# Two more projections of a decoder layer join the seven-product stage of the gates, and the memory norm moves

## The chip, the cores and the metric

The kernel runs on one core of a Trainium2 chip. The metric is the device time of one launch in microseconds (us), lower is better. The engines named below: PE multiplies matrices (TensorE; its weight loads are listed as PEld), DVE works on vectors (VectorE), ACT evaluates functions and scaled copies (ScalarE), POOL is the general engine (GpSimd), SP issues most DMAs. PE writes to PSUM banks, from which ACT or DVE take the results. Each engine works through its own queue in order and waits on semaphores for the others.

## The reference, cut to what matters

One layer of a decoder on 1024 tokens of width 1024, float32. After a feed-forward half step, one input projection gives u, v (512 columns each), the latent parts of branch B, q_mem (512) and three gates (1024 each). Branch A gates u spatially with v, branch B is causal latent attention, branch C attends to 256 memory tokens with 4 heads of 128; the gated branches are projected and added, and a second feed-forward half step follows.

```
h = rmsnorm(x, mix_norm)
z = h @ w_in                     # [u | v | c_q | c_kv | k_rope | q_mem | gate_A | gate_B | gate_C]
u = gelu(z[..., u]);  v = layernorm(gelu(z[..., v]))
y_a = u * (tril(w_s) @ v + b_s)  # in chunks of 128 tokens, 8 groups of 64 columns
q   = rmsnorm(z[..., q_mem] by head, q_norm)
kv  = rmsnorm(mem, mem_norm) @ w_kv;  k = rmsnorm(kv[:512] by head, k_norm);  v = kv[512:]
y_c = softmax(q k^T * 128**-0.5) v
gates  = sigmoid(z[..., gates] + b_gate)
merged = gates_A*(y_a @ w_branch_a) + gates_B*(y_b @ w_branch_b) + gates_C*(y_c @ w_branch_c)
```

## The kernel before

**Products.** Every large product is three PE matmuls (`mm3`, L141): each operand is split into a high part (an ACT cast, L127) and a low part (a DVE subtraction, L128), and hi·hi, hi·lo and lo·hi are added in one PSUM bank. A product needs the low part too, so it waits for ACT and then DVE.

**Seven products for four.** The feed-forward layers and the gates go through class `Seven`, which makes a 2x2 block product from seven block products instead of eight, and pays with additions of blocks on DVE and POOL. In the gates' stage (`Gates`) a unit is two blocks of 128 columns over all tokens and takes 84 matmuls of 512 columns; 12 units make the 3 x 8 gate blocks. `emit` applies a sigmoid and stores each finished block, features in partitions and tokens along the row, to DRAM (`gate`).

**After the gates**, `mixer` runs latent attention's projections, then `sgu`: for each half of the tokens v (96 matmuls, `gelu_rows`), its Gelu on ACT and its LayerNorm on DVE (L625 to L631; its inverse root is a chain of small Newton steps, `rs_y`, L154 to L165); then for each half u (96 matmuls more), the spatial product with `sg_w` (24 matmuls of 256 columns), `u <- (product + b) * u` on DVE (L643) and 16 transposes with a split into `x4`. Tokens stand in partitions until those transposes.

**Memory.** `mem_kv` loads the memory into `m_x`, sums its squares (`norm_feed`, `token_sums`), takes the root, spreads it over the partitions with two transposes (`norm_scale`) and scales and splits it (`norm_put`: L399, then L127 and L128 for `m_hi` and `m_lo`). Between these steps `fill` advances `branch_a`, a generator of branch A's 16 output products (12 matmuls each). Two products give keys and values (96 matmuls each). `mem_attention` makes q_mem by rows of 128 tokens (`zrow`, 8 times 24 matmuls), norms its heads (`head_norm`), transposes them (4 of 128x128 for each row), and runs scores, Exp, transposes and values for pairs of rows, with branch A's products in between (`F`).

**Order.** Inside these functions the order on each engine is made at build time by a scheduler from the program's order and modelled times, and is fixed on the chip. A tile with n buffers makes a new writer wait until the readers of the nth writer before it are through.

Of the kernel before, what the change touches and what calls it, by code (L numbers as in the profile page):

```python
# [34 lines left out]
ML = 256  # L35
EPS = 1e-6
# [6 lines left out]
class Kernel:  # L43
# [154 lines left out]
    def constants(self):  # L198
        nc, const = self.nc, self.const
        self.ident = const.tile([P, P], F32, name="ident")  # L200
        make_identity(nc, self.ident)
        self.ones = const.tile([P, 1], F32, name="ones")
        nc.gpsimd.memset(self.ones, 1.0)
        warm = const.tile([P, 1], F32, name="warm")
        nc.scalar.activation(warm, self.ident[:, :1], ACT.Silu)
# [394 lines left out]
    def sgu(self, h):  # L600
        nc, a, tc = self.nc, self.a, self.tc
        with tc.tile_pool(name="sgu", bufs=1) as p:
# [11 lines left out]
            vs = []  # L614
            for hf in range(2):
                vhi, vlo = (p.tile([P, 4, SGW], F32R, name=n, bufs=2) for n in ("v_hi", "v_lo"))
# [34 lines left out]
        return yt  # L651
# [17 lines left out]
    def mem_kv(self, p, filler):  # L669

        nc, a, tc = self.nc, self.a, self.tc
        kt = tuple(p.tile([P, MH, ML], F32R, name=n) for n in ("mk_hi", "mk_lo"))
        vv = tuple(p.tile([P, 2, MH * MD], F32R, name=n) for n in ("mv_hi", "mv_lo"))
        with tc.tile_pool(name="memkv", bufs=1) as q:
            mt = tuple(q.tile([P, DT, ML], F32R, name=n) for n in ("m_hi", "m_lo"))
            x = q.tile([P, DT, ML], F32, name="m_x")
            nc.sync.dma_start(x, a["mem"])
            def fill(n):
                for _ in range(n):
                    next(filler)  # L680

            fill(2)
            acc = None
            for c in range(DT):
                acc = self.norm_feed(acc, x[:, c], ML, late=c == 0)
            fill(2)
            r = self.rms(self.token_sums(acc, late=True), ML // P, D)
            fill(3)
            scale = self.norm_scale(r, late=True)
            for c in range(DT):  # L690
                self.norm_put(mt[0][:, c], mt[1][:, c], x[:, c], self.g_mem[:, c:c + 1], scale)
            fill(1)

            def product(w):
                ps = self.mm()
                for d in range(DT):
                    for i in range(2):
                        s = tuple(x[:, d, i * P:(i + 1) * P] for x in mt)
                        self.mm3(ps[:, i], s, w[d], d == 0, d == DT - 1)
                return ps  # L700

            ps = product(self.load(a["mem_w_kv"][0]))
            w = self.load(a["mem_w_kv"][1])
            x = q.tile([P, 2, MH, MD], F32, name="m_k")
            self.head_norm(x, [ps[:, 0], ps[:, 1]])
            ps = product(w)
            for hh in range(0, MH, 2):
                self.to_feature(
                    tuple(t[:, hh:hh + 2].rearrange("p h m -> p (h m)") for t in kt),
                    [x[:, t, hh + k] for k in range(2) for t in range(2)], self.mk_g,  # L710
                )
# [1224 lines left out]
```

## Time and profile before

| what | us |
|---|---|
| three runs of the kernel | 2201.34, 2201.59, 2202.05 |
| their median | 2201.59 |
| span of the profiled execution | 2198.6 |

The profiled execution's span counts from its first to its last instruction and is 3.0 us under the runs' median. In a table of stretches a row gives the stretch, its length, and the busy time and count of instructions of PE, PEld, DVE, ACT and POOL, then the granted clock of PE (1.00 is full), the DMA share and GB/s. In a timeline a row gives start, duration, engine, line, operation, output and inputs, shapes and count, and in brackets the idle time before it with what ended it. In a table of groups, count, total and mean ns, idle time before and its releasers follow the bar or the shapes. DMA rows end with KB of each and the median us from issue to landing.

### The profile page before, as it was taken

How to read it: one execution, taken by the hardware profiler on the slowest of the kernel's cores; microseconds unless marked ns; L12 is line 12 of the kernel's file. 1: busy time of each engine (PE TensorE's matmuls, PEld its weight loads, DVE VectorE, ACT ScalarE, POOL GpSimd, SP SyncE). 2: the span in 40 equal slices, each digit the busy share in tenths (PEclk: the TensorE clock that was granted, in tenths of full speed). 3: DMA queues.
4: the chain of work that ended last, by engine and by line, in shares of the span. 5: the costliest groups of instructions: out<-in, count | busy, mean ns of one | idle time of the engine just before them, and what ended most of it. 6: DMA issues, size and time to landing. Idle time of an engine off the chain costs nothing.

```text
span 2198.6 us, 27597 instructions
## 1 busy us (share of the span) xinstructions
PE 2181.6 (99%) x10304; PEld 1819.9 (83%) x10304; DVE 1549.2 (70%) x2415; ACT 896.7 (41%) x1501; POOL 243.8 (11%) x246
## 2 busy tenths in 40 slices
PE   9999999999999999999999999999999999999999
PEld 5788888888887888898888889988888888888887
DVE  7966666679889555467466769885886666657884
ACT  5422222243455333444244559843432222234332
POOL 0012112100000000022000221140011111210000
PEclk9999999999999999999999999999999999999999
DMA  4242333385432333225151541094033333338543
GB/s 145 82 146 99 96 101 115 133 306 172 133 114 96 125 106 125 94 92 172 55 190 58 218 175 43 17 332 166 29 124 100 99 109 101 115 116 299 170 130 106
DMA packets 113062, 285.92 MB, mean 130 GB/s; under 512 B 13344, under 2 KB 21664, under 8 KB 112800
## 3 DMA queue, kind: packets, MB, share of 16 engines
q1 hardware_dynamic: 112928, 284.16, 38.0%
q8 instruction: 81, 1.33, 0.2%
q14 instruction: 53, 0.43, 0.1%
HBM read 201.80 MB, written 82.31 MB: 129 GB/s over the span
## 4 chain that ended last, share of the span: by engine, by line
PE 93%; DVE 5%; ACT 1%; issue 1%; DMA 0%; SPq 0%; ACTq 0%; DVEq 0%
PE bank L144 13%; PE bank L145 13%; PE bank L146 13%; PE one L144 13%; PE one L145 13%; PE one L146 13%; PE mm L146 3%; PE mm L144 3%; PE mm L145 3%; PE bank L879 1%; PE bank L415 1%; PE bank L894 1%; PE bank L895 1%; DVE wlo L133 1%; PE one L1579 1%
## 5 line engine op out<-in xcount | busy, mean ns | idle before, releaser
L132 ACT CAST whi<-x 128x1024 fp32r<-128x1024 f32 (+1 forms) x189 | 179.5, 952 | 469.8 <-PE one L145 206.8
L1283 DVE TENSOR_TENSOR t<-t,one 128x512 f32<-128x512 f32 x178 | 122.2, 686 | 229.5 <-PE one L146 228.7
L144 PE MATMUL bank<-h,whi 128*128 128x512 f32 x644 | 250.9, 390 | 0.0
L145 PE MATMUL bank<-h,whi 128*128 128x512 f32 x644 | 250.7, 389 | 0.0
L146 PE MATMUL bank<-h,wlo 128*128 128x512 f32 x644 | 250.5, 389 | 0.0
L133 DVE TENSOR_TENSOR wlo<-x,whi 128x1024 fp32r<-128x1024 f32 (+1 forms) x189 | 226.2, 1198 | 28.6 <-ACT whi L132 28.5
L144 PE MATMUL one<-h,whi 128*128 128x512 f32 x476 | 186.2, 391 | 0.7 <-ACT t L1392 0.7
L146 PE MATMUL one<-h,wlo 128*128 128x512 f32 x476 | 185.2, 389 | 0.0
L145 PE MATMUL one<-h,whi 128*128 128x512 f32 x476 | 185.2, 389 | 0.0
L127 ACT CAST whi<-w 128x1024 fp32r<-128x1024 f32 (+1 forms) x108 | 95.1, 899 | 143.4 <-PE one L145 62.7
L128 DVE TENSOR_TENSOR wlo<-w,whi 128x1024 fp32r<-128x1024 f32 (+1 forms) x108 | 110.1, 1033 | 60.5 <-ACT whi L127 60.4
L144 PE MATMUL one<-w,whi 128*128 128x512 f32 x392 | 152.5, 389 | 0.0
L145 PE MATMUL one<-w,whi 128*128 128x512 f32 x392 | 152.5, 389 | 0.0
L146 PE MATMUL one<-w,wlo 128*128 128x512 f32 x392 | 152.5, 389 | 0.0
L1680 POOL TENSOR_TENSOR raw<-raw 128x512 f32<-128x512 f32 x38 | 62.6, 1647 | 804.3 <-DVE raw L1526 804.3
L146 PEld LDWEIGHTS bank<-h,wlo 128*128 128x128 f32 x644 | 120.9, 188 | 25.1
L144 PEld LDWEIGHTS bank<-h,whi 128*128 128x128 f32 x644 | 120.9, 188 | 24.9
L145 PEld LDWEIGHTS bank<-h,whi 128*128 128x128 f32 x644 | 120.9, 188 | 24.8
L144 PE MATMUL bank<-whi 128*128 128x512 f32 x352 | 136.9, 389 | 0.0
L145 PE MATMUL bank<-wlo,whi 128*128 128x512 f32 x352 | 136.9, 389 | 0.0
L146 PE MATMUL bank<-whi,wlo 128*128 128x512 f32 x352 | 136.9, 389 | 0.0
L128 DVE TENSOR_TENSOR wlo<-h,whi 128x512 fp32r<-128x512 f32 x130 | 88.2, 714 | 25.7 <-ACT whi L127 25.7
(381 smaller groups left out, 5040.1 us busy)
## 6 DMA issues: line engine op xcount, KB each, us to landing
x<-in_ffn_w_gu_dram SPq DMA_DIRECT2D x78, 512.0 KB, 5.1
w<-tdt SPq DMA_DIRECT2D x40, 512.0 KB, 4.8
tdb<-raw SPq DMA_DIRECT2D x64, 256.0 KB, 2.1
h<-in_ffn_w_down_dram SPq DMA_DIRECT2D x64, 256.0 KB, 6.0
w<-tdb SPq DMA_DIRECT2D x30, 512.0 KB, 4.5
tdt<-w SPq DMA_DIRECT2D x48, 256.0 KB, 2.1
gate<-raw SPq DMA_DIRECT2D x23, 512.0 KB, 2.6
tdt<-raw SPq DMA_DIRECT2D x40, 256.0 KB, 2.9
```

Of the source, the lines that this page charges most:

```text
L127: self.nc.scalar.copy(hi, src)
L128: return (eng or self.nc.vector).tensor_tensor(lo, src, hi.bitcast(F32), op=ALU.subtract)
L132: self.nc.scalar.copy(hi, src)
L133: return lambda: self.nc.vector.tensor_tensor(lo, src, hi.bitcast(F32), op=ALU.subtract)
L144: mmul(out, s[0], m[0], start=first, stop=False, **kw)
L145: mmul(out, s[0], m[1], start=False, stop=False, **kw)
L146: self.last = mmul(out, s[1], m[0], start=False, stop=last, **kw)
L415: nc.tensor.transpose(b[:m, k * P:(k + 1) * P], s, self.ident)
L879: nc.tensor.transpose(b[:, at:at + P], prs[t][:, kk * P:(kk + 1) * P], self.ident)
L894: nc.tensor.matmul(o, w, pt[0], start=n == 0, stop=False)
L1283: return self.nc.vector.tensor_tensor(out, x, y, op=ALU.add)
L1680: sub = lambda d, x, y: (eng or nc.gpsimd).tensor_tensor(d, x, y, op=ALU.subtract)
```

## The change

u and q_mem become blocks 24 to 31 of the gates' stage: 16 units instead of 12, in the same table of weights. `emit` copies q_mem's blocks, applies Gelu to u's, and stores both to DRAM in the layout of the gates. `sgu` no longer computes u: the spatial product gets its bias on ACT (`Identity`) into `m`, `m` is transposed, and the stored u block is loaded and multiplied by it, features in partitions.

q_mem is loaded with features in partitions, so it needs no transposes. Its root mean square is not applied to q: squares (ACT), an addition (POOL) and 16 products with a selector of two columns (`pick`) give the sums for each token and head; the root enters as the scale of Exp, and multiplies the row minimum.

The memory norm is cut in two: squares and sums (`mem_norm`) are issued between v's halves, the rest (`finish`) behind v's second half, and `mem_kv` follows at once, ahead of the spatial gating. `mem_kv` no longer advances `branch_a`; the generator is used in `mem_attention` alone, in a new sequence.

```diff
+ZQ = 3 * DT
+ZU = ZQ + MH
+ZB = ZU + SGW // P
@@ sgu
+            vs, norm = [], None
             for hf in range(2):
+                if hf:
+                    norm = self.mem_norm()
...
-            w = self.load(a["w_u"])
+            kv = self.mem_kv(norm())
             yt = [self.split_pair() for _ in range(4)]
             for hf in range(2):
-                u, v = p.tile([P, 4, SGW], F32, name="u"), vs[hf]
-                self.gelu_rows(u, h[hf], w, hf == 0)
+                m, v = p.tile([P, 4, SGW], F32, name="u"), vs[hf]
                 for g in range(SGG):
...
-                    nc.vector.scalar_tensor_tensor(
-                        u[:, :, cols], in0=b, scalar=self.sg_b[:, g:g + 1], in1=u[:, :, cols],
-                        op0=ALU.add, op1=ALU.mult)
+                    nc.scalar.activation(m[:, :, cols], b, ACT.Identity, bias=self.sg_b[:, g:g + 1])
                 for j in range(4):
-                    self.to_feature(
-                        tuple(t[:, hf * 512:hf * 512 + 512] for t in yt[j]),
-                        [u[:, c, j * P:(j + 1) * P] for c in range(4)],
-                    )
+                    u = self.row()
+                    nc.sync.dma_start(u, self.z[ZU + j][:, hf])
+                    b = self.bank()
+                    for c in range(4):
+                        nc.tensor.transpose(b[:, c * P:(c + 1) * P], m[:, c, j * P:(j + 1) * P], self.ident)
+                    nc.vector.tensor_tensor(u, u, b, op=ALU.mult)
+                    self.split(*(t[:, hf * 512:hf * 512 + 512] for t in yt[j]), u)
@@ mem_norm
+        acc = None
+        for c in range(DT):
+            acc = self.norm_feed(acc, x[c], ML)
+        hi, lo = views(2, F32R), views(2, F32R)
+        def finish():
             r = self.rms(self.token_sums(acc, late=True), ML // P, D)
             scale = self.norm_scale(r, late=True)
             for c in range(DT):
+                self.norm_put(hi[c], lo[c], x[c], self.g_mem[:, c:c + 1], scale)
+            return hi, lo
@@ mem_queries
+        for pair in range(MH // 2):
+            sq = [p.tile([P, S], F32, name="m4", bufs=3) for n in range(2)]
+            for o in range(2):
+                q = self.raw()
+                nc.sync.dma_start(q, self.z[ZQ + 2 * pair + o].rearrange("p a w -> p (a w)"))
+                qt.append(tuple(p.tile([P, S], F32R, name=n, bufs=MH) for n in ("mq_hi", "mq_lo")))
+                for n, t in enumerate(sq):
                     nc.scalar.activation(
+                        t[o * P // 2:(o + 1) * P // 2], q[n * P // 2:(n + 1) * P // 2], ACT.Square)
+                self.split_gain(*qt[-1], q, gq)
+            nc.gpsimd.tensor_tensor(sq[0], sq[0], sq[1], op=ALU.add)
+            for t in range(NT):
+                at = t * MH + 2 * pair
+                nc.tensor.matmul(b[:, at:at + 2], sq[0][:, t * P:(t + 1) * P], self.pick, start=True, stop=True)
+        r = p.tile([P, NT * MH], F32, name="mq_r")
+        nc.vector.tensor_copy(r, self.rms(b, NT * MH, MD))
...
@@ mem_attention, scores
+            nc.vector.tensor_tensor(mx, mx, r[:, at:at + MH], op=ALU.mult)
...
+                    pr[:, hh], sc[:, hh], ACT.Exp, bias=mx[:, hh:hh + 1], scale=nr[:, at + hh:at + hh + 1],
...
+        for f, *x in ((F,), (F,), (F,), (S, 0, 0), (S, 0, 1), (F,), (T, 0, 0), (S, 1, 0), (F,), (T, 0, 1), (S, 1, 1),
+                      (F,), (V, 0), (T, 1, 0), (F,), (S, 2, 0), (T, 1, 1), (F,), (S, 2, 1), (F,), (V, 1), (T, 2, 0),
+                      (F,), (S, 3, 0), (T, 2, 1), (F,), (S, 3, 1), (F,), (V, 2), (T, 3, 0), (F,), (T, 3, 1), (F,),
+                      (F,), (V, 3)):
@@ mixer
-        ya = self.sgu(h)
-        branch_a = self.branches(0, ya, sink_a)
+        ya, kv = self.sgu(h)
         with tc.tile_pool(name="mem", bufs=1) as p:
-            kv = self.mem_kv(p, branch_a)
-            yc = self.mem_attention(h, *kv, branch_a)
+            branch_a = self.branches(0, ya, sink_a)
+            queries = self.mem_queries(p)
+            yc = self.mem_attention(p, queries, *kv, branch_a)
@@ Gates.emit
-        self.nc.scalar.activation(d, ps, ACT.Sigmoid, bias=k.b_gate[:, n:n + 1])
+        if n < ZQ:
+            self.nc.scalar.activation(d, ps, ACT.Sigmoid, bias=k.b_gate[:, n:n + 1])
+        elif n >= ZU:
+            self.nc.scalar.activation(d, ps, ACT.Gelu)
+        elif row is None:
+            self.nc.scalar.copy(d, ps)
```

The order on PE where v's second half ends, before (`bank_8090` is v, `mm_8284` the first u product of 96 matmuls):

```order
L144 MATMUL bank_8090<-whi_7923,h4_5162 128x512
L145 MATMUL bank_8090<-wlo_7924,h4_5162 128x512
L146 MATMUL bank_8090<-whi_7923,h4_5163 128x512
L144 MATMUL mm_8284<-whi_8245,h4_6690 128x512
L145 MATMUL mm_8284<-wlo_8246,h4_6690 128x512
L146 MATMUL mm_8284<-whi_8245,h4_6691 128x512
```

And in the changed kernel (`bank_8647` is v, `t_8614` the memory's sum of squares, `rs_y_8805` its inverse root, `h4_8637` and `h4_8639` the high and low parts of the normalised memory, `mm_8880` and `mm_8986` keys and values):

```order
L147 MATMUL bank_8647<-whi_8449,h4_5174 128x512
L148 MATMUL bank_8647<-wlo_8450,h4_5174 128x512
L149 MATMUL bank_8647<-whi_8449,h4_5175 128x512
L380 MATMUL bank_8800<-ones_91,t_8614 128x1 x2
L392 MATMUL bank_8817<-ident_86,rs_y_8805 128x128 x2
L147 MATMUL mm_8880<-whi_8850,h4_8637 128x512
L148 MATMUL mm_8880<-wlo_8851,h4_8637 128x512
L147 MATMUL mm_8986<-whi_8931,h4_8637 128x512
L148 MATMUL mm_8986<-wlo_8932,h4_8637 128x512
L149 MATMUL mm_8880<-whi_8850,h4_8639 128x512
```

The u product has gone from behind v, and the memory's norm and products have come up to that place.

The order on DVE at the same place, in the changed kernel (`rs_y_8756` and `rs_y_8782` belong to LayerNorm of v's second half, `rs_y_8805` to the memory; `u_8643` is v, `h4_8610` and `h4_8611` the memory):

```order
L168 SCALAR_TENSOR_TENSOR rs_y_8782<-rs_b_8784,rs_y_8782 128x2
L640 SCALAR_TENSOR_TENSOR u_8643<-u_8643,rs_y_8756,ln_b_8414 128x512 x2
L168 SCALAR_TENSOR_TENSOR rs_y_8805<-rs_b_8807,rs_y_8805 128x2
L640 SCALAR_TENSOR_TENSOR u_8643<-u_8643,rs_y_8782,ln_b_8414 128x512 x2
L406 SCALAR_TENSOR_TENSOR h4_8610<-h4_8610,c_mem_norm_3203,bank_8817 128x256 x4
L406 SCALAR_TENSOR_TENSOR h4_8611<-h4_8611,c_mem_norm_3203,bank_8817 128x256
L131 TENSOR_TENSOR v_lo_8642<-u_8643,v_hi_8641 128x1024
L406 SCALAR_TENSOR_TENSOR h4_8611<-h4_8611,c_mem_norm_3203,bank_8817 128x256 x3
L131 TENSOR_TENSOR v_lo_8642<-u_8643,v_hi_8641 128x1024
L131 TENSOR_TENSOR h4_8639<-h4_8610,h4_8637 128x256 x4
L131 TENSOR_TENSOR h4_8640<-h4_8611,h4_8638 128x256 x4
```

Before, the memory's part of this stood among branch A's steps (`t_8806` and `t_8856` are theirs):

```order
L955 TENSOR_TENSOR t_8806<-t_8806,bank_8808 128x512
L399 SCALAR_TENSOR_TENSOR m_x_8638<-m_x_8638,c_mem_norm_3199,bank_8823 128x256 x8
L128 TENSOR_TENSOR m_lo_8637<-m_x_8638,m_hi_8636 128x256 x4
L955 TENSOR_TENSOR t_8856<-t_8856,bank_8858 128x512
L128 TENSOR_TENSOR wlo_8900<-raw_8897,whi_8899 128x512 x2
L128 TENSOR_TENSOR m_lo_8637<-m_x_8638,m_hi_8636 128x256 x4
```

The memory's low parts now come after both low parts of v, and no step of branch A stands near.

The order on ACT behind the spatial gating, in the changed kernel (`u_9140` is `m` of the second half, `raw_9230`, `raw_9238`, `raw_9257` and `raw_9265` the four q blocks, `x4` branch A's operand):

```order
L651 ACTIVATE u_9140<-bank_9176,c_sg_b_3207 128x4x64
L130 CAST x4_9051<-t_9181 128x512
L745 ACTIVATE m4_9228<-raw_9230 64x1024
L745 ACTIVATE m4_9229<-raw_9230 64x1024
L130 CAST x4_9053<-t_9191 128x512
L139 ACTIVATE mq_hi_9232<-raw_9230,m_gq_9225 128x1024
L745 ACTIVATE m4_9228<-raw_9238 64x1024
L745 ACTIVATE m4_9229<-raw_9238 64x1024
L139 ACTIVATE mq_hi_9240<-raw_9238,m_gq_9225 128x1024
L745 ACTIVATE m4_9255<-raw_9257 64x1024
L139 ACTIVATE mq_hi_9259<-raw_9257,m_gq_9225 128x1024
L130 CAST x4_9055<-t_9201 128x512
```

PE's rows of the same place, from the last head's scores on (`mm_9377` and `mm_9402` are the first two score tiles, `bank_9322` branch A's first step):

```order
L147 MATMUL mm_9377<-h4_8844,mq_hi_9267 128x256
L148 MATMUL mm_9377<-h4_8845,mq_hi_9267 128x256
L147 MATMUL mm_9402<-h4_8844,mq_hi_9267 128x256
L148 MATMUL mm_9402<-h4_8845,mq_hi_9267 128x256
L149 MATMUL mm_9377<-h4_8844,mq_lo_9268 128x256
L149 MATMUL mm_9402<-h4_8844,mq_lo_9268 128x256
L147 MATMUL bank_9322<-x4_9051,whi_9310 128x512
```

The queries, which PE made itself before, row by row, now come from ACT and DVE, and the first step of branch A stands behind the scores of all four heads.

More of the change, by code (lines that the diff above doesn't have):

```diff
@@ L702, in mem_kv @@
[L702 to L711, printed above, removed]
@@ L1063, in run @@
             gates.run(x1d, r0)
-            self.sig = gates.z
+            self.sig = self.z = gates.z
         with self.banks("mixps") as self.pm:
@@ L1457, in __init__ @@
         super().__init__(k, w, pool, norm)
-        self.z = [k.dram.tile([P, 2, 512], F32, name=f"gate{i}") for i in range(3 * DT)]
+        self.z = [k.dram.tile([P, 2, 512], F32, name=f"gate{i}") for i in range(ZB)]
         self.o, self.w0 = {}, {}
```

192 lines of the change are left out of this document (93 added, 99 removed).

## The prediction

> **What bounds the kernel now.** I read the page's busy shares first, then the chain that ended last, then a table of stretches of the part that the change rewrites (between latent attention's projections and the end of memory attention).
>
> ```profile
> span 2198.6 us, 27597 instructions
> PE 2181.6 (99%) x10304; PEld 1819.9 (83%) x10304; DVE 1549.2 (70%) x2415; ACT 896.7 (41%) x1501; POOL 243.8 (11%) x246
> PE 93%; DVE 5%; ACT 1%; issue 1%; DMA 0%; SPq 0%; ACTq 0%; DVEq 0%
> 1042.00:1070.00 28.00, 27.70 (x140) 23.35 (x140) 19.55 (x52) 8.91 (x13) 0.00 (x0) 1.00 0.07 20
> 1070.00:1120.00 50.00, 49.54 (x239) 41.15 (x237) 24.13 (x55) 15.15 (x32) 0.00 (x0) 1.00 0.48 152
> 1120.00:1205.00 85.00, 84.16 (x428) 71.44 (x428) 55.39 (x122) 39.05 (x90) 0.00 (x0) 1.00 0.31 100
> ```
>
> PE is busy 99% of the span and is 93% of the chain; in the three stretches (u and gating; memory keys and values; memory attention; columns length, then PE, PEld, DVE, ACT, POOL busy, granted clock, DMA) it idles 0.30, 0.46 and 0.84 us. So a matmul removed here is worth its full issue step, and a wait that nothing covers costs its full length. All sums below are on this execution's axis; its span is 3.0 us under the runs' median of 2201.59, which I add at the end.
>
> **Removed and added work.** Steps between starts give the price of PE work that keeps pace:
>
> ```profile
> 1042.06 0.39 PE L144 MATMUL mm<-whi,h 128*128 128x512 f32 x1
> 1046.82 0.39 PE L144 MATMUL mm<-whi,h 128*128 128x512 f32 x1
> 957.99 0.60 PE L415 MATMUL bank<-ident,l_xs 128*128 128x128 f32 x4
> 1063.82 0.28 PE L144 MATMUL bank<-v_hi,x 128*128 128x256 f32 x1
> 1065.01 0.28 PE L145 MATMUL bank<-v_lo,x 128*128 128x256 f32 x1
> ```
>
> The first two rows are 21 matmuls apart: 4.76/21 = 0.227 us for 512 columns. The last two are 10 apart: 0.119 for 256. Four transposes in 0.60, of which about 0.27 is the tail of the last, give 0.11 each. u and q_mem took 2x96 + 8x24 = 384 matmuls of 512 columns; four units of 84 take 336. So 48 go, 10.9 us; 32 query transposes go, 3.5; 16 products of two columns come, at most a transpose's price, 1.8. Net -12.6. With the old stretches' own idle time, 0.30+0.46+0.84 = 1.6, the ceiling of the gain is **14.2 us**. The four units stand in the gates' stage, at whose end PE waits for nothing (205 us busy of 205) while DVE and ACT have time left:
>
> ```profile
> 700.00:905.00 205.00, 205.00 (x910) 169.90 (x909) 113.91 (x152) 82.31 (x114) 0.00 (x0) 1.00 0.39 131
> ```
>
> so I take the four at this step and at no other cost; their copies, Gelus and stores go to ACT and to queues that the twelve already use.
>
> **Hole 1: nothing is left behind v.** Before, the u product (96 matmuls, 21.8 us) follows v's second half, and branch A's products surround the memory norm. Now PE's next rows are two token sums, two transposes of rs_y and the memory products, which need m normalised and split. These rows set the price:
>
> ```profile
> 1025.89 1.28 ACT L591 ACT_TABLE_LOAD   x1 [15.74 <-DMA qd<-q]
> 1040.43 1.29 DVE L128 TENSOR_TENSOR wlo<-raw,whi 128x512 fp32r<-128x512 f32 x2
> 1041.64 2.36 DVE L128 TENSOR_TENSOR v_lo<-u,v_hi 128x1024 fp32r<-128x1024 f32 x2
> 1044.66 1.29 DVE L625 BATCH_NORM_STATS2 bn<-u 128x6 f32<-128x512 f32 x2
> 1050.09 0.24 DVE L154 TENSOR_SCALAR rs_y<-rms_v 128x2 int32<-128x2 int32 x2
> 1051.66 0.23 DVE L165 SCALAR_TENSOR_TENSOR rs_y<-rs_b,rs_y 128x2 f32<-128x2 f32 x2
> 1051.86 2.74 DVE L631 SCALAR_TENSOR_TENSOR u<-u,rs_y,ln_b 128x512 f32<-128x512 f32 x4
> 1054.52 2.43 DVE L128 TENSOR_TENSOR v_lo<-u,v_hi 128x1024 fp32r<-128x1024 f32 x2
> 1053.31 1.05 ACT L127 CAST v_hi<-u 128x1024 fp32r<-128x1024 f32 x1 [7.21 <-DVE u L631]
> 1117.33 3.22 DVE L399 SCALAR_TENSOR_TENSOR m_x<-m_x,c_mem_norm,bank 128x256 f32<-128x256 f32 x8
> 1117.84 1.58 ACT L127 CAST m_hi<-m_x 128x256 fp32r<-128x256 f32 x4 [2.92 <-DVE m_x L399]
> 1120.46 1.42 DVE L128 TENSOR_TENSOR m_lo<-m_x,m_hi 128x256 fp32r<-128x256 f32 x4
> ```
>
> DVE's new order, on that axis. The first half's v_lo ended at 44.0 (all +1000); Gelu's table load now happens in the gates' stage, so it ends at 42.7, and two weight splits (1.29) follow: 44.0. LayerNorm's statistics up to the first rs_y take 1050.09-1044.66 = 5.43: 49.4. Its two chains and that of the memory norm now alternate, 27 instructions at (1051.86-1050.09)/18 = 0.098: 52.1. Two LayerNorm products of 0.68: 53.4. The memory's rs_y, then two transposes on PE: about 54.1, while DVE does two more products: 54.9. Five m_x at 0.40: 56.9; a v_lo of 1.2: 58.1; three m_x: 59.3; the other v_lo: 60.5; the first m_lo, 0.36: 60.85. Here PE resumes; before that it can only run the sums, the transposes and four hi products (ACT's m_hi come behind its two v_hi), 1.35 us. From 1042.06 the idle time is 18.8-1.35 = **17.4 us**. The low bound, with the two v_lo (2.4) off the path and half of the alternation hidden (1.4), is 13; the high one, with one later v_hi and a DVE gap for each hand-over, 20. The eight keys' transposes behind the products cost nothing: V's last 38 matmuls (8.6 us) cover the head norm.
>
> **Hole 2: gating halves back to back.** Before, each half's gating had a u product ahead of it. Now 48 matmuls of 256 columns and 32 transposes run with four banks, each emptied by ACT, then DVE:
>
> ```profile
> L751 ACT ACTIVATE h<-mm,m_mx 128x256 f32<-128x256 f32 x24 | 11.1, 481 | 3.0 <-DVE m_mx L746 3.0
> L127 ACT CAST whi<-bank 128x512 fp32r<-128x512 f32 x16 | 8.6, 594 | 1.5 <-PE bank L797 1.5
> L955 DVE TENSOR_TENSOR t<-t,bank 128x512 f32<-128x512 f32 x16 | 10.9, 683 | 5.0 <-PE bank L146 3.0 <-PE bank L373 1.5 <-DMA t<-gate 0.5
> ```
>
> PE alone needs 48x0.119 + 32x0.11 = 9.2. ACT needs 16 Identities, at 0.395 (the m_hi row's 1.58/4) to 0.48, with four casts of 0.57 between them; the last transposes wait for the last Identity, and DVE empties each bank of transposes in 0.68. Followed through in order that is about 12.3 at the low price, so **3.1**; 5 at the high one, 1 if the casts fall behind the Identities.
>
> **Hole 3: queries.** Program order has three branch-A steps ahead of the scores; the order on PE has all 24 matmuls of the first two score tiles first, with each head waiting for its mq_hi and mq_lo. No Square of 64 partitions is in this trace; the nearest row has 128:
>
> ```profile
> 1027.18 1.94 ACT L591 ACTIVATE u<-mm 128x1024 f32<-128x1024 f32 x2
> L127 ACT CAST v_hi<-u 128x1024 fp32r<-128x1024 f32 x4 | 4.2, 1055 | 9.1 <-DVE u L631 9.1
> L128 DVE TENSOR_TENSOR v_lo<-u,v_hi 128x1024 fp32r<-128x1024 f32 x4 | 4.8, 1221 | 0.0
> x<-gate SPq DMA_DIRECT2D x12, 512.0 KB, 7.3
> raw<-in_mem_w_kv_dram SPq DMA_DIRECT2D x8, 512.0 KB, 3.6
> ```
>
> Count from gating's last transpose. ACT's first cast of the second half ends 0.1 before it; then two Squares (0.97 each), a cast (0.57), mq_hi (1.05) end at 3.5, and four more Squares, three more mq_hi and two casts follow in its queue to 11.6; DVE's last mq_lo to 12.8. The fourth q block reuses the first's buffer, free at 4.7 (after its mq_lo): by 3.6 us it lands at 8.3, ahead of its first reader at 9.6, and by 7.3 us at 12.0, which adds 2.4. PE has 24x0.119 + 8x0.11 = 3.8 us for these 12.8: 9.0 idle, and the first branch weights, whose splits stand behind this on ACT and DVE, cost a wlo and a whi, about 1.3. Together **10.3**. Low bound, with Squares at half price because half of the partitions work and half of the casts ahead: 6; high, with the slow load and a DVE queue ahead of mq_lo: 16.
>
> The Trainium skill ("ScalarE: Activation LUTs", What ACT_TABLE_LOAD costs) gives an activation's time by elements for each lane, so a Square of 64 partitions would cost what one of 128 does: this speaks for the middle value; no row here shows it.
>
> The rest of memory attention costs nothing extra: per pair of tiles PE has 24 matmuls of 256, 8 transposes and 1.5 branch steps of 12x0.227, 7.8 us, and DVE 1.22 for the minimum, 1.22 for the normalising, and splits, about 7.0. If that cover fails, 8 pairs by some 0.5 us make 4.
>
> **Clock.** After a PE wait at the start of the run the granted clock fell:
>
> ```profile
> 14.51 1.05 PE L373 MATMUL bank<-ones,t 128*128 128x1 f32 x8 [1.25 <-DVE t L1128]
> 12.00:16.00 4.00, 2.75 (x12) 1.59 (x12) 2.63 (x5) 1.80 (x4) 0.00 (x0) 0.93 1.01 366
> 16.00:20.00 4.00, 4.00 (x10) 1.54 (x9) 3.63 (x14) 1.94 (x3) 0.00 (x0) 0.65 1.06 405
> ```
>
> A mean of 0.93 and then 0.65 over 4 us each is a loss of 0.28+1.40 = 1.7 us of full-speed work after 1.25 us of idling. Holes 1 and 3 are each longer. At least 1.7 apiece, and what the waking engine loses in its first stretch beside it: **4.0** for both; bounds 0 (no fall) and 7 (hole 2 as well).
>
> The Trainium skill ("TensorE: Matmul & The Clock Gate", The HAM clock gate) has the clock halved after an idle window of about 3.4 us and restored after a busy window as long. It speaks against this change; by it hole 1 surely pays and hole 3, where scattered matmuls run, perhaps not: 2 in place of 4. The trace shows the fall after less idling than that.
>
> **Sum.** -12.6 -1.6 +17.4 +3.1 +10.3 +4.0 = +20.6. Span 2219.2, runs about **2222**.
>
> **Rivals.**
> A, faster: the holes stay covered and the matmul count decides. For it: ACT is busy 41% and DVE 70%, so each chain could be done early if its engine got to it in time. Against: the orders on DVE and PE are fixed in the program, and hole 1's shortest reading, 13, alone nearly repays 14.2. With no hole, 2201.6-14.2 = 2187; it is faster than a measurement can tell (0.2%, 4.4 us) only where holes and clock sum to less than 9.8. Chance 0.07; about even, 0.03.
> B, only hole 1: the queries are prepared while PE is still in gating, since their loads need only z; hole 3 leaves 1.3. Then 2222-9-2 = 2211 or a little less. For it: q blocks 1 to 3 have free buffers. Against: ACT's rows put the Squares behind gating's casts. 0.15.
> C, longer: the fourth q load takes 7.3 us or more and the first branch weights behind it come late too, and memory attention becomes DVE-bound: 2222+2.4+4+4 = 2232 or more. 0.12.
>
> **Numbers.** The forecast (2214 to 2229 by its own terms' bounds taken halfway) has 0.63. The range 2208 to 2233 takes in B and the short end of C. Slower by over 0.2%: 0.90; within: 0.03; faster: 0.07.
>
> **What would show it.** In the changed kernel's trace: after v's last matmul a PE idle of 13 to 20 us, released by DVE's m split; DVE's two v_lo between m_x rows; a wait of PE on mq_lo and mq_hi in the scores, the last near 13 us behind gating's transposes; a granted clock well under 1 in the 4 us after each; the gates' stage some 76 us longer (336x0.227) with its idle time unchanged. I am wrong if PE has other rows to run in hole 1, if the queries are ready when gating ends, or if the four added units wait for their loads or stores.

## The result, and the profile after

The changed kernel takes 2222.74 us (median of 4 runs, 2221.93 to 2223.71), the kernel before 2201.71 (4 runs beside it, 2201.34 to 2202.05): a ratio of 1.0095, 95% interval 1.0083 to 1.0108. It is 21.0 us slower. The profiled executions differ by 22.6 us (spans of 2221.2 and 2198.6); the account below is made on these two.

One slip above: each of the two products for keys and values takes 48 matmuls, 96 together.

From the page of the changed kernel, the span, the busy times and the chain:

```profile
span 2221.2 us, 27585 instructions
PE 2183.0 (98%) x10256; PEld 1819.3 (82%) x10256; DVE 1563.5 (70%) x2406; ACT 913.1 (41%) x1513; POOL 249.8 (11%) x252
PE 89%; DVE 7%; ACT 2%; issue 1%; DMA 1%; POOL 0%; SPq 0%; ACTq 0%; DVEq 0%; POOLq 0%
```

PE has 48 instructions fewer and yet 1.4 us more of busy time, and the chain now runs through DVE for 7% where it was 5%. The table of stretches says where (columns as before: length, then PE, PEld, DVE, ACT, POOL busy, granted clock, DMA share, GB/s):

```profile
700.00:1000.00 300.00, 300.00 (x1381) 251.17 (x1380) 162.55 (x232) 112.64 (x171) 1.73 (x6) 1.00 0.35 119
1119.40:1122.10 2.70, 0.27 (x3) 0.17 (x2) 2.70 (x4) 1.95 (x4) 0.00 (x0) 1.00 0.62 197
1122.10:1142.58 20.48, 7.74 (x20) 5.55 (x21) 18.49 (x65) 6.06 (x13) 0.00 (x0) 0.50 0.08 26
1142.60:1160.00 17.40, 17.40 (x78) 14.37 (x78) 8.15 (x19) 5.48 (x10) 0.00 (x0) 1.00 0.56 182
1160.00:1172.90 12.90, 12.18 (x91) 11.00 (x90) 8.24 (x13) 10.27 (x23) 0.00 (x0) 1.00 0.15 43
1172.90:1192.00 19.10, 12.15 (x51) 10.34 (x50) 13.58 (x14) 16.84 (x19) 4.74 (x2) 0.64 0.55 177
1192.00:1262.00 70.00, 69.79 (x417) 61.34 (x416) 52.87 (x97) 36.10 (x102) 2.60 (x3) 1.00 0.49 162
```

The gates' stage (first row), with its four added units, has no idle PE. From 1119 to 1143 PE works 8 us of 23 while DVE is nearly always busy, and the clock is at half for 20.5 us; keys and values then run at full pace; the spatial gating loses little; from 1173 to 1192 PE works 12 of 19 us and ACT 17. PE's timeline at the first place (start, duration, engine, line, operation, names, shapes, count, and in brackets the idle time before and what ended it):

```profile
1119.12 0.39 PE L149 MATMUL bank<-whi,h 128*128 128x512 f32 x1
1121.94 0.89 PE L380 MATMUL bank<-ones,t 128*128 128x1 f32 x4 [2.43 <-ACT u L598]
1131.33 0.66 PE L392 MATMUL bank<-ident,rs_y 128*128 128x128 f32 x2 [8.51 <-DVE rs_y L168]
1133.95 0.80 PE L147 MATMUL mm<-whi,h 128*128 128x512 f32 x1 [1.95 <-ACT h L130]
1138.30 0.80 PE L149 MATMUL mm<-whi,h 128*128 128x512 f32 x1 [2.28 <-DVE h L131]
```

The last matmul of v, the memory's sums, the spread of its root, the first hi products, and the first product that needs a low part: four waits, 15.2 us. DVE's rows of the same time say why:

```profile
1122.38 1.28 DVE L634 BATCH_NORM_STATS2 bn<-u 128x6 f32<-128x512 f32 x2
1127.80 0.16 DVE L157 TENSOR_SCALAR rs_y<-rms_v 128x2 int32<-128x2 int32 x1
1129.71 1.41 DVE L640 SCALAR_TENSOR_TENSOR u<-u,rs_y,ln_b 128x512 f32<-128x512 f32 x2
1131.03 0.15 DVE L168 SCALAR_TENSOR_TENSOR rs_y<-rs_b,rs_y 128x2 f32<-128x2 f32 x1
1132.43 2.04 DVE L406 SCALAR_TENSOR_TENSOR h<-h,c_mem_norm,bank 128x256 f32<-128x256 f32 x5
1134.39 1.21 DVE L131 TENSOR_TENSOR v_lo<-u,v_hi 128x1024 fp32r<-128x1024 f32 x1
1136.70 1.21 DVE L131 TENSOR_TENSOR v_lo<-u,v_hi 128x1024 fp32r<-128x1024 f32 x1
```

LayerNorm's statistics come first, the memory's root ends at 1131.2, two LayerNorm products stand ahead of its multiplications, and v's two low parts between and behind these. At the second place ACT makes the queries, and PE waits for each head (ACT's timeline, then PE's):

```profile
1173.63 2.12 ACT L745 ACTIVATE m<-raw 64x1024 f32<-64x1024 f32 x2
1176.30 1.14 ACT L139 ACTIVATE mq_hi<-raw,m_gq 128x1024 fp32r<-128x1024 f32 x1
1184.87 1.15 ACT L139 ACTIVATE mq_hi<-raw,m_gq 128x1024 fp32r<-128x1024 f32 x1
```

```profile
1177.50 0.58 PE L147 MATMUL mm<-h,mq_hi 128*128 128x256 f32 x1 [3.95 <-ACT mq_hi L139]
1180.81 0.58 PE L147 MATMUL mm<-h,mq_hi 128*128 128x256 f32 x1 [1.20 <-ACT mq_hi L139]
1183.17 0.80 PE L149 MATMUL mm<-h,mq_lo 128*128 128x256 f32 x2 [1.13 <-DVE mq_lo L140]
1183.77 3.41 PE L751 MATMUL bank<-pick,m 128*128 128x2 f32 x16
1191.23 0.50 PE L149 MATMUL bank<-x,wlo 128*128 128x512 f32 x1 [0.57 <-DVE wlo L131]
```

The Squares stand ahead of the casts to mq_hi in ACT's queue, so the first score row starts 4 us late and the fourth head is not there until 1186.

### The profile page after: what moved, and what is told of

It is laid out like the page before. It is cut to its first block, busy times and chain, and to the rows that moved or that the text cites. A ratio compares the mean times of both kernels' runs of the same rounds, so it can differ in the third digit from the quotient of the medians.

```text
span 2221.2 us, 27585 instructions
## 1 busy us (share of the span) xinstructions
PE 2183.0 (98%) x10256; PEld 1819.3 (82%) x10256; DVE 1563.5 (70%) x2406; ACT 913.1 (41%) x1513; POOL 249.8 (11%) x252
## 4 chain that ended last, share of the span: by engine, by line
PE 89%; DVE 7%; ACT 2%; issue 1%; DMA 1%; POOL 0%; SPq 0%; ACTq 0%; DVEq 0%; POOLq 0%
PE one L147 14%; PE one L148 14%; PE one L149 14%; PE bank L147 12%; PE bank L149 12%; PE bank L148 12%; PE mm L149 2%; PE mm L147 2%; PE mm L148 2%; PE bank L902 1%; PE bank L917 1%; PE bank L918 1%; DVE wlo L131 1%; PE bank L422 1%; DVE wlo L136 1%
## 5 line engine op out<-in xcount | busy, mean ns | idle before, releaser
L135 ACT CAST whi<-x 128x1024 fp32r<-128x1024 f32 (+1 forms) x201 | 191.2, 954 | 501.9 <-PE one L148 220.4
L147 PE MATMUL bank<-h,whi 128*128 128x512 f32 x676 | 263.3, 390 | 0.0
L148 PE MATMUL bank<-h,whi 128*128 128x512 f32 x676 | 263.1, 389 | 0.0
L149 PE MATMUL bank<-h,wlo 128*128 128x512 f32 x676 | 263.0, 389 | 0.0
L136 DVE TENSOR_TENSOR wlo<-x,whi 128x1024 fp32r<-128x1024 f32 (+1 forms) x201 | 239.7, 1194 | 31.7 <-ACT whi L135 31.6
L147 PE MATMUL one<-h,whi 128*128 128x512 f32 x508 | 198.7, 391 | 0.7 <-ACT t L1414 0.7
L149 PE MATMUL one<-h,wlo 128*128 128x512 f32 x508 | 197.7, 389 | 0.0
L148 PE MATMUL one<-h,whi 128*128 128x512 f32 x508 | 197.7, 389 | 0.0
L147 PE MATMUL one<-w,whi 128*128 128x512 f32 x424 | 164.9, 389 | 0.0
L149 PE MATMUL one<-w,wlo 128*128 128x512 f32 x424 | 164.9, 389 | 0.0
L148 PE MATMUL one<-w,whi 128*128 128x512 f32 x424 | 164.9, 389 | 0.0
L148 PEld LDWEIGHTS bank<-h,whi 128*128 128x128 f32 x676 | 126.9, 188 | 26.2
L147 PEld LDWEIGHTS bank<-h,whi 128*128 128x128 f32 x676 | 126.9, 188 | 26.2
L147 PEld LDWEIGHTS one<-h,whi 128*128 128x128 f32 x508 | 95.4, 188 | 21.0 <-ACT t L1414 1.1
```

What stands on the lines that cost most here:

```text
L135: self.nc.scalar.copy(hi, src)
L136: return lambda: self.nc.vector.tensor_tensor(lo, src, hi.bitcast(F32), op=ALU.subtract)
L147: mmul(out, s[0], m[0], start=first, stop=False, **kw)
L148: mmul(out, s[0], m[1], start=False, stop=False, **kw)
L149: self.last = mmul(out, s[1], m[0], start=False, stop=last, **kw)
```

## The experiments

Twelve kernels. Each ratio is to the kernel before, run beside it, with its 95% interval; "the changed kernel" is the one above, at 2222.74.

**Memory norm inside v's second half** (`e1_norm_in_v`). The sums go behind the third, the transposes of the root behind the fourth of eight blocks of v's second half, and DVE does the memory's normalising ahead of LayerNorm:

```diff
-                self.gelu_rows(rows, h[hf], w, hf == 0)
+                self.gelu_rows(room, h[hf], w, hf == 0, {2: norm[0], 3: lambda: (norm[1](), ln0())} if hf else {})
...
+                            if not hf:
+                                self.after(b, norm[3][0])
```

> The memory norm's sums, root, spreading and splits are put inside v's second half (sums after its third of eight steps, spreading after the fourth), and DVE does them ahead of LayerNorm of v's first half; all else as in the changed kernel. Theory (the hole behind v is a chain that only starts its second part when PE has nothing left): PE's idle time between v and the memory products goes from 16.3 us to under 2 and the granted clock stays at 1 there (another 3.2), so 2222.7 - 16.3 - 3.2 + 1 = about 2204, range 2201 to 2208. Rival (DVE's total work behind v's first half is the bound, not its order): LayerNorm of the second half comes late instead, PE waits before the spatial gating, and the time is 2212 to 2223.

2211.45 us, 1.0044 (1.0030 to 1.0057): 11.3 us off the changed kernel, short of the theory's 2204. Hole 1 is gone: PE has no wait of over 0.4 us until the one below, behind the products of keys and values (PE's timeline, then the stretch up to it):

```profile
1148.98 1.30 PE L427 MATMUL bank<-ident,h 128*128 128x128 f32 x5 [7.36 <-DVE h L700]
```

```profile
1106.00:1149.00 43.00, 35.64 (x161) 29.20 (x160) 40.86 (x128) 18.93 (x34) 0.00 (x0) 0.95 0.39 130
```

The transposes of the keys wait for the head norm's multiplication, which stands behind LayerNorm of v's second half on DVE. DVE is busy 40.9 of 43 us, so another order on it could give back little more. This is the wait that the rival names, with a time just under the rival's range.

**Three branch steps ahead of the queries** (`e2_fill_queries`):

```diff
             branch_a = self.branches(0, ya, sink_a)
+            for _ in range(3):
+                next(branch_a)
             queries = self.mem_queries(p)
...
-        for f, *x in ((F,), (F,), (F,), (S, 0, 0),
+        for f, *x in ((S, 0, 0),
...
```

> Three branch-A steps are issued ahead of the queries' preparation in place of behind it, all else as in the changed kernel; PE's order then has 36 matmuls of 512 columns (8.2 us) between gating's last transposes and the first scores. Theory (the wait for mq_hi and mq_lo is only uncovered): the 12.8 us lost there, idle time and lowered clock together, fall to 3 or 4, so about 2222.7 - 9 = 2213.5, range 2211 to 2217. Rival (ACT is the bound of the whole stretch, so the wait comes back at the first Exp and transposes): 2219 to 2223.

2219.36, 1.0079 (1.0064 to 1.0095): the rival. The waits for mq_hi are gone, and this one has come (PE's timeline, then ACT's and DVE's):

```profile
1199.33 0.58 PE L147 MATMUL mm<-h,mq_hi 128*128 128x256 f32 x1 [6.88 <-ACT m L778]
```

```profile
1195.68 1.28 ACT L778 ACT_TABLE_LOAD   x1 [7.71 <-DVE m_mx L774]
```

```profile
1190.70 2.35 DVE L773 TENSOR_REDUCE m_mx<-mm 128x4 f32<-128x1024 f32 x2
1195.21 0.18 DVE L753 COPY mq_r<-rs_y 128x32 f32<-128x32 f32 x1
```

The third score tile needs the bank of the first, which is free when its four Exps are done; these need the row minima, the root (a chain up to 1195.4), and a table load. The three steps that used to cover this had been moved.

**Both edits** (`e3_both`):

> The two moves together. Theory: they touch different places and add up, 2222.7 - 18.5 - 9 = about 2195, range 2192 to 2199, below the 2201.7 of the kernel before the change: what the change was worth without its holes. Rival (the queues' order behind one fixed hole makes the next): no better than the kernel before, 2201 or more.

2212.28, 1.0045 (1.0032 to 1.0057): the rival, no better than the first alone; PE waits 8.6 us for the keys and 6.9 for the Exps.

**Dummy matmuls in hole 1** (`e4_keep_busy`). 52 unused matmuls keep PE busy during its waits (8, 36 and 8):

```diff
...
+                    i = nc.tensor.matmul(warm[:, 0], h[1][7][0][:, :P], w[7][0], start=True, stop=True)
...
```

> The changed kernel with 52 extra matmuls of 512 columns whose result is not used, put into the hole behind v (8 ahead of the token sums, 36 ahead of the transposes, 8 behind them): the hole stays as long, but PE is busy in most of it. Theory (the fall of the granted clock costs about 3.2 us behind the hole, apart from its length): clock 1 through the stretch, 2222.7 - 3.2 = about 2219.5, range 2218 to 2221. Rival (the clock does not follow PE's idle time, or the slow matmuls were hidden): no change, 2222 to 2224.

2222.73, 1.0094 (1.0080 to 1.0108). Inconclusive: the dummies ended 3.3 us early, and the clock fell in that wait after all. So again with 24 in place of the last 8 (`e5_keep_busy_to_the_end`):

> As e4, with 24 unused matmuls in place of 8 behind the transposes (68 in all), so that PE is busy up to the moment at which the first low part of the memory is due; in e4 the clock held through the hole but fell in the last 3.6 us of idling, just ahead of the products. Theory (what costs is the half clock that the products meet, about 4 us of them): the clock stays at 1 until the scores, 2222.7 - 3 = about 2219.7, range 2218 to 2221. Rival (the products are paced by DVE and ACT there and the half clock hides): 2222 to 2224.

2220.87, 1.0088 (1.0075 to 1.0102), 1.9 us off the changed kernel and inside the theory's range. This row of stretches stands against 7.74 us of work at 0.50 in the changed kernel:

```profile
1117.00:1142.00 25.00, 23.94 (x106) 18.79 (x105) 24.28 (x73) 10.30 (x20) 0.00 (x0) 1.00 0.07 22
```

At full clock throughout, the hole still costs nearly all it did: the half clock behind it is worth 1 to 2 us.

**The root early** (`e6_early_root`). Squares, sums and root are made during keys and values, with the three steps ahead as above; q is loaded twice for it:

```diff
+        roots = self.mem_roots()
...
-            queries = self.mem_queries(p)
+            queries = self.mem_queries(p, roots)
```

> The changed kernel with the queries' squares, sums and root made while PE works on memory keys and values, and three branch-A steps ahead of the queries' split; q is loaded a second time for the split. e2 showed the wait for the queries' split replaced by one of 7 us for the Exp, which wants the root. Theory (hole 3 is two chains on ACT, split and root, and closes only when both are covered): 2222.7 - 12.8 + 1 = about 2211, range 2209 to 2214. Rival (squares on ACT, additions on POOL and second loads collide with the keys' chain or the gating, or memory attention is bound by DVE from the start): 2216 or more.

2224.71, 1.0106 (1.0092 to 1.0119): no faster than the changed kernel (2.0 us above it, with intervals that overlap), as the rival has it. Hole 1 is as it was; PE's waits at the queries (total, times, longest):

```profile
PE mm L147 <- ACT m L788: 6.6, 1, 6.6
PE bank L747 <- POOL h L744: 3.1, 2, 3.0
```

The wait for the Exps is the same with the root made early, so the root's chain isn't its only cause: here the minima, the table load and the Exps make it without the root. The picks now wait for POOL's sums in a place with no cover.

**All of it, with POOL's help** (`e7_all_covered`). The first edit, the early root, and half of DVE's splits of the key weights and all of the value weights' on POOL; the keys' transposes behind the first half's gating:

```diff
-        ps = product(self.load(a["mem_w_kv"][0]))
-        w = self.load(a["mem_w_kv"][1])
+        ps = product(self.load(a["mem_w_kv"][0], pool=(1, 3, 5, 7)))
+        w = self.load(a["mem_w_kv"][1], pool=(0, 1, 2, 3, 4, 5, 6, 7))
```

> e1 and e6 together, with three more moves: the low parts of the memory's weights for values, and half of those for keys, are made by POOL in place of DVE; v's second half is written to buffers of its own, so the first half's gating need not wait for it; the keys' transposes and the root stand behind the first half of the gating. e1 showed DVE as the next bound (PE 7.5 us idle at the keys' transposes). Theory (each hole was a chain that could be covered, and DVE's load behind v was the last of them): no PE idle time over 2 us and clock 1 between v and the scores, 2222.7 - 19.5 - 12.8 - 1.5 + 2 = about 2191, range 2189 to 2197, below the kernel before. Rival (DVE is full in that stretch, and sharing with POOL slows it): 2200 or more.

2214.69, 1.0061 (1.0048 to 1.0074): the rival's side. And without the early root and the moved steps (`e8_hole1_covered`):

> e7 without the early root and without the branch-A steps ahead of the queries: hole 1 and its follower are covered, hole 3 is left as in the changed kernel. Theory: 2222.7 - 19.5 - 1 + 1 = about 2203, range 2201 to 2206, and e7 lies below it by hole 3's 12. Rival (what is gained behind v is lost again ahead of the gating, as in e1): 2209 to 2213.

2214.66, 1.0062 (1.0046 to 1.0077), above both ranges and no better than the first edit alone; PE now waits for v's parts ahead of the gating (2.5 us for one low part), as the rival has it. POOL and DVE of the first of the two, in time:

```profile
1121.68 11.86 POOL L132 TENSOR_TENSOR wlo<-raw,whi 128x512 fp32r<-128x512 f32 x8 [2.27 <-ACT whi L131]
1137.66 2.43 POOL L785 TENSOR_TENSOR h<-h,h 128x1024 f32<-128x1024 f32 x1 [4.12 <-ACT h L783]
```

```profile
1122.62 0.66 DVE L659 BATCH_NORM_STATS2 bn<-h 128x6 f32<-128x512 f32 x1
1123.20 1.57 DVE L665 SCALAR_TENSOR_TENSOR u<-u,mv,ln_g 128x512 f32<-128x512 f32 x1
1125.86 1.87 DVE L665 SCALAR_TENSOR_TENSOR u<-u,mv,ln_g 128x512 f32<-128x512 f32 x1
1137.74 2.36 DVE L165 SCALAR_TENSOR_TENSOR rs_w<-rs_b,rms_v 128x2 f32<-128x2 f32 x1
```

DVE's products of two SBUF operands take 1.57 and 1.87 us beside POOL's in place of 0.7, and an operation on two columns, of 0.15 us elsewhere, ends with POOL's add; the statistics, with one operand, keep their 0.66. Not every operation of one operand does: two on two columns (`rms_v`) took 1.25 and 1.16 us in the same stretch. The Trainium skill ("GPSIMD Engine Reference", Specifications) has POOL's SBUF interfaces shared with VectorE, with contention for DVE instructions of two SBUF inputs or in a 2-port mode; the rows above agree for two inputs, and no run here shows the mode of the others. Work that POOL takes off DVE this way comes back, at least in part, as longer DVE rows. How much of the time that is, no run separates: these two kernels also move the keys' transposes and give v's second half buffers of its own.

**Steps on both sides of the scores** (`e9_steps_both_sides`), in the changed kernel, three ahead of the queries and three ahead of the first turn:

```diff
-        for f, *x in ((F,), (F,), (F,), (S, 0, 0), (S, 0, 1), (F,), (T, 0, 0),
+        for f, *x in ((S, 0, 0), (S, 0, 1), (F,), (F,), (F,), (T, 0, 0),
...
```

> e2 with the branch-A steps laid out again: three ahead of the queries' preparation as in e2, and three, not one, behind the first two score tiles; nothing else differs from the changed kernel. In e2, e6 and e7 alike the third score tile waited 6.6 to 7.0 us for the first tile's PSUM, that is for the row minimum on DVE, a table load and Exp on ACT, whether the root was early or not. Theory (hole 3 is two latencies in a row, the split ahead of the scores and the softmax behind them; the changed kernel's steps covered the second by chance of the order, e2 covered the first instead): both covered, 2222.7 - 12.8 + 3 = about 2213, range 2210 to 2216. Rival (ACT's and DVE's work is the bound, and PE waits again later): 2217 or more.

2219.06, 1.0080 (1.0064 to 1.0095): the rival, with a wait of 6.4 us for the Exps as in the second experiment.

**The same with the first edit** (`e10_dve_order_and_steps`), LayerNorm of v's second half ahead of gating's multiplications on DVE, the keys' transposes behind the first half's gating, and v's second half in buffers of its own; no POOL:

> e1 and e9 together; against e7 the low parts of the weights are back on DVE, the queries' root is back in its place, and LayerNorm of v's two halves is kept in order on DVE, ahead of the gating's multiplications. In e7 DVE instructions took 1.2 to 2.4 us in place of 0.1 to 0.7 where POOL's ran beside them. Theory (DVE's order and not POOL is the cure, and DVE's load up to LayerNorm's end, some 3 us after PE is through with the first half's gating, is what remains): 2222.7 - 19.5 + 3.5 - 10 = about 2197, range 2193 to 2202. Rival (DVE is behind by more, as in e1): 2203 or more.

2207.32, 1.0029 (1.0017 to 1.0040): 15.4 us off the changed kernel, but short of 2197, and so the rival. Two waits of over 0.5 us are left, as PE's timeline shows, with the picks ahead of the second:

```profile
1152.89 1.97 PE L427 MATMUL bank<-ident,h 128*128 128x128 f32 x8 [7.33 <-DVE t L689]
1182.97 1.84 PE L795 MATMUL bank<-pick,m 128*128 128x2 f32 x16
1191.22 0.58 PE L148 MATMUL mm<-h,mq_hi 128*128 128x256 f32 x1 [6.41 <-ACT m L822]
```

This shows what the earlier kernels had hidden. The last picks, on which the root, the table load and the Exps hang, stand on PE behind the 72 matmuls of six steps: the cover is spent before the chain that needs it starts.

**The picks first** (`e12_picks_first`), on top of that. Three steps stay ahead of the queries; one more stands ahead of the last picks, and three behind them and ahead of the third score tile, held there by order (seven in all, where the kernel above had six):

```diff
-        for f, *x in ((S, 0, 0), (S, 0, 1), (F,), (F,), (F,), (T, 0, 0), (S, 1, 0), (F,),
+        for f, *x in ((Q, 0, 0), (Q, 0, 1), (F,), (B, 1), (F,), (F,), (F,), (E, 0, 0), (E, 0, 1), (B, 0), (S, 1, 0),
+                      (T, 0, 0), (F,),
...
```

(Q and E are the products and the softmax of a tile; B holds the next matmul behind the picks, or behind the last step.)

> The kernel of e10_dve_order_and_steps, with the last pick matmuls held ahead of three of branch A's steps, these steps held ahead of the third score tile, and the softmax of the first two tiles written behind them. The theory: the 6.4 us wait of the third score tile in e10 (6.41 <- ACT m) is an order: the last picks stood behind 72 matmuls of the steps, so the root, the table load and the first Exps came 8 us late, and PE had nothing left while they ran. With some 36 matmuls (8.2 us) behind the picks the wait falls to at most 2 us (what the picks then wait for is GpSimd's sum), and the half clock behind it goes or shrinks; from e10's 2207.3 that is 2201 us (2199 to 2204). The rival: the work of the steps is only moved, and the wait returns at the picks or at later score tiles that have lost their cover: 2205 us or more.

2200.78, 0.9992 (0.9983 to 1.0000): the theory, at its middle. PE's two waits of over 0.5 us that are left there:

```profile
1153.24 1.97 PE L430 MATMUL bank<-ident,h 128*128 128x128 f32 x8 [7.31 <-DVE t L692]
1178.77 1.95 PE L798 MATMUL bank<-pick,m 128*128 128x2 f32 x16 [1.01 <-POOL m L795]
```

**LayerNorm's sums on ACT** (`e13_sums_on_act`), added to that:

```diff
-                            b = nc.vector.bn_stats(st[:, k], v[:, k])
...
-                            nc.vector.bn_aggr(mv[:, k], st[:, k])
...
+            nc.scalar.activation(d, ps[i // 2][:, i % 2] if pairs else ps[i], ACT.Gelu, accum_out=ls[:, i:i + 1])
...
+                            nc.scalar.activation(
+                                self.row(), rows(i)[:, k], ACT.Square, accum_out=lq[:, i + k:i + k + 1])
```

> The kernel of e12_picks_first, with the LayerNorm's statistics as sums on ScalarE (the Gelu's accumulated sum, and a Square with an accumulated sum per row of 128x512) in place of VectorE's batch statistics. The theory: VectorE's work sets the 7.4 us wait of the keys' transposes in e10; eight statistics of 0.62 us and eight aggregates of about 0.09 us leave it (5.6 us) and some twelve small operations of 0.08 to 0.16 us come (1 to 1.5 us); the wait falls to 2 to 4 us, and the time by 4 us against e12_picks_first, to 2197 us (2194 to 2201), which is below the kernel before. The rival: ScalarE's casts, now behind eight Squares of 0.6 us and as many reads of the sums, set the same wait, or VectorE's order does: within 1.5 us of e12_picks_first, or slower.

2197.75, 0.9979 (0.9970 to 0.9988): 3.0 us off the last one, 25.0 off the changed kernel, and faster than the kernel before (2202.25, 21 runs beside it). The stretch up to the keys' transposes in the kernel that keeps the statistics (`e10_dve_order_and_steps`), then in this one:

```profile
1106.00:1153.00 47.00, 39.62 (x194) 33.17 (x195) 45.36 (x134) 24.02 (x45) 0.00 (x0) 0.95 0.39 130
```

```profile
1106.00:1150.00 44.00, 39.80 (x194) 32.88 (x193) 41.13 (x105) 29.23 (x66) 0.00 (x0) 1.00 0.42 142
```

And this one's wait in PE's timeline, and its busy times on the page:

```profile
1150.00 1.25 PE L430 MATMUL bank<-ident,h 128*128 128x128 f32 x8 [1.99 <-DVE t L701]
```

```profile
PE 2171.4 (99%) x10256; PEld 1811.5 (82%) x10256; DVE 1558.9 (71%) x2376; ACT 919.9 (42%) x1539; POOL 249.1 (11%) x252
```

DVE has 4.2 us less to do, ACT 5.2 more, and PE's wait falls from 7.3 to 2.0: DVE's sum of work had set it. ACT wasn't the limit. Not all of these 5.3 us come off the time: two waits that `e12_picks_first` does not have appear, 1.55 us for the memory's root (at 1110.97) and 1.40 at a branch step (at 1189.25), both on DVE. With the same 10256 instructions PE's busy time is 11.6 us under the changed kernel's, whose slow clock it lacks, and 10.2 under the kernel before: close to what the account below has for the removed matmuls.

## Why the prediction was right, and where its sizes were off

2222 was predicted, with 2208 to 2233 as its range; 2222.74 came. The account on the two profiled executions, in us:

| term | predicted | found |
|---|---|---|
| matmuls removed and added | -12.6 | -10.8 |
| idle time of the old stretches | -1.6 | -2.0 |
| hole 1 | +17.4 | +17.4 |
| gating halves back to back | +3.1 | +2.0 |
| hole 3, queries | +10.3 | |
| clock, behind holes 1 and 3 | +4.0 | +2.1 behind hole 1 |
| hole 3 with its clock | | +12.8 |
| a clock fall near the start | 0 | +0.8 |
| sum | +20.6 | +22.3 |

The found ones come from PE's steps between starts against the steps at full pace; the other 0.3 of the 22.6 had come by 40 us.

The mechanism was right, but that 2222 lies within 1 us of the median is in part luck. Behind holes 1 and 3 the price of the waits was 2.5 too low and that of the clock up to 1.9 too high; the matmuls gave back 1.8 less than forecast, and gating cost 1.1 less. And the medians differ by 21.0, these two executions by 22.6.

- **Matmuls.** The count was wrong in one place. The 16 picks are 32 instructions in the trace (the row of 16 above is one pair of heads, as the memory's two sums are four), so they cost 32 by 0.11 = 3.6 and not 1.8. 10304 - 10256 = 48 instructions agree: 48 products and 32 transposes gone, 32 come.
- **Hole 1.** From v's last row to the first product with a low part are 19.2 us. Taking off its own step (0.23) and what PE did between (four sums, two transposes, four products, 1.57 at full pace) leaves 17.4. DVE's order was read right, and its statistics took 5.42 us to the first rs_y (5.43 predicted). It began 1.1 us later than worked out (3.0 us behind v's end, not 1.9), and the alternating chains gave most of that back (1.9 us in steps of 0.07, where 2.7 in steps of 0.098 were taken), so it is partly luck that the two figures are the same.
- **Who pays.** The first experiment and the last two show the cause: PE's order had no other row there, and with other rows it doesn't wait. The dummies show that the waiting, not the clock, is most of the price.
- **Gating.** 2.0, under the middle value of 3.1 and within its bounds of 1 and 5.
- **Hole 3.** The order (Squares and casts of gating ahead of mq_hi) and the price of a Square were right. The group of the Squares in the changed kernel (count, total, mean ns):

```profile
L745 ACT ACTIVATE m<-raw 64x1024 f32<-64x1024 f32 x8 | 8.4, 1052 | 0.1
```

  That is 1052 ns on 64 partitions, beside 1055 for a cast on 128, as the Trainium skill ("ScalarE: Activation LUTs", What ACT_TABLE_LOAD costs) counts it by elements for each lane; the low bound at half price falls. What the sum left out is POOL. DVE's rows in the changed kernel:

```profile
1180.80 3.51 DVE L140 SCALAR_TENSOR_TENSOR mq_lo<-raw,m_gq,mq_hi 128x1024 fp32r<-128x1024 f32 x2 [2.03 <-ACT mq_hi L139]
1188.85 2.32 DVE L131 TENSOR_TENSOR wlo<-raw,whi 128x512 fp32r<-128x512 f32 x1 [1.51 <-ACT whi L130]
```

  The first of these two mq_lo took 2.32 us where one alone takes 1.28, and the low part of branch A's first weight 2.32 where the next ones take 0.68; both began while POOL was adding squares (1179.66 to 1182.03 and 1188.25 to 1190.62), as in the experiment with POOL. The second is what PE's last wait, at 1191.23, ends on: up to 1.6 us of the 2.5 that the term lacked.
- **Clock.** The clock fell in both holes, to half for 20.48 and 13.65 us, with PE busy 7.7 and 10.4 of them. Behind hole 1 that cost 2.1 us. Behind hole 3 the rows show no price of its own: ACT works without a pause from 1173.6 to 1188.8, and PE then waits for the low part that DVE makes from ACT's last cast, so PE at full clock would have waited longer for the same row. That is read from the rows; no run holds the clock up there. The prediction's 1.7 for each hole did not hold for hole 3.
- **Rivals.** The faster kernel (A) needed covered holes; it takes the edits of the last two experiments. That only hole 1 opens (B) is refuted by PE's rows at the queries. The long load (C) didn't come, as this row of DMA issues shows (size, then median from issue to landing); the fourth head was late by ACT's queue, not by its load:

```profile
raw<-gate SPq DMA_DIRECT2D x4, 512.0 KB, 3.5
```

What the prediction left out is what hole 3 hid: with the queries covered, the softmax of the first tiles is the next wait. It named memory attention's cover as a risk of 4 us; the experiments met waits of 6.4 to 6.9 us at one place, once the queries were covered.

## What to carry to other kernels

A change that takes matmuls from a bound PE is worth them only if nothing that they covered comes bare: before removing a product, list the chains of other engines that ran behind it. When cover is put back, look at where it stands against the first instruction of the chain, not only at its amount: here six branch steps ahead of the last picks left a wait of 6.4 us, and with four ahead and three behind it was gone. When the wait then moves to an engine that is busy throughout the stretch, take work from that engine, and give it to one beside which its other instructions keep their length: DVE's grew beside POOL's, and when ACT took the statistics DVE's busy time fell by 4.2 us.

## What the runs showed of the hardware that was not expected

- The clock fell just behind waits of 2.0 to 2.4 us, and not each time: near 70 us both kernels wait the same 2.0 us, and only the changed one has half clock behind it, for 3.41 us (first row below, of the changed kernel's stretches); of the twelve kernels of the experiments, four have it there too. The half-clock times are multiples of that: 3.41, 13.65, 20.48. The Trainium skill ("TensorE: Matmul & The Clock Gate", The HAM clock gate) counts activity in a free-running window of 3.4 us and has the clock fall after an idle one; the multiples agree with that, falls after 2.0 to 2.4 us of waiting don't.

```profile
70.80:74.21 3.41, 3.41 (x9) 2.68 (x9) 3.41 (x5) 2.42 (x4) 0.00 (x0) 0.50 0.00 0
1176.72:1190.37 13.65, 10.44 (x42) 9.26 (x42) 9.21 (x8) 11.94 (x14) 4.48 (x2) 0.50 0.55 171
```

- It stayed at half for 13.65 us with PE busy 10.4 of them (the last row, at the queries): work with short gaps doesn't bring it back at once.
- Two columns cost as much as 128: each of the two instructions of a pick takes about 0.11 us of PE at full clock (1.84 for the 16 of a pair of heads), and so does a transpose of 128 columns.
